# A two-layer hybrid decoder on one core: the first half of a down projection moved into column block 2, with one quad more as seven products

## The chip, the core and the metric

The kernel runs on one core of a Trainium2 chip (trn2). The metric is device time in microseconds of one launch, the median of several runs; lower is better. In the text TensorE is PE, VectorE is DVE, ScalarE is ACT, GpSimd is POOL, and SyncE is SP. Weights reach the core through two DMA queues, one fed by SP and one fed by POOL.

## What is computed

Two layers, each with a token mixer (sparse attention and latent attention side by side, one output projection) and a SwiGLU feed-forward part, each followed by a layer norm. 256 tokens, model width 2048, feed-forward width 5632, all in float32. The change lies in the feed-forward part, which is

```python
def _swiglu(x, w_gate, w_up, w_down):
    h = jax.nn.silu(jnp.einsum('bsd,df->bsf', x, w_gate)) * jnp.einsum('bsd,df->bsf', x, w_up)
    return jnp.einsum('bsf,fd->bsd', h, w_down)

def reference(...):
    for i in range(DEPTH):
        mix = _hybrid_mixer(x, positions, ...)
        x = _layer_norm(ALPHA * x + mix, ln1_g[i], ln1_b[i])
        ffn = _swiglu(x, w_gate[i], w_up[i], w_down[i])
        x = _layer_norm(ALPHA * x + ffn, ln2_g[i], ln2_b[i])
    return x
```

## The kernel before

**Three products for one.** Every float32 operand is split into a high and a low part. A weight unit is a tile of 128 partitions by 1024 (two 128-row steps of K, 512 columns; 512 KB). `load_raw` (L317) brings it in on SP's queue, `parts` makes `wh` from it on ACT (L344) and the remainder `wl` on DVE (L345), and PE takes three products for each pair of token tile and K step: high by high, high by low, low by high. So one unit with one token tile is 2 x 3 = 6 matmuls of 512 columns. There are seven buffers for a pair of `wh` and `wl` in the feed-forward part (`UNITS` 5 and `MORE` 2): unit number n+7 waits until PE has finished with unit n.

**Column blocks.** The feed-forward width is cut into 11 column blocks of 512. Block 0 is computed plainly (`gu`), blocks 1 to 10 by `gate_up`. Gate and up together form a 2 x 2 problem (two token tiles, two column sets), and K is cut into four pairs of units, called quads. A quad is computed in one of three ways, named by a letter in `ORDER`:

- N, `plain_quad`: eight products of 6 matmuls, four units.
- S, `wino_quad`: seven products of 6 matmuls (a Strassen-Winograd scheme). Seven `wh`/`wl` pairs are made; four of them are of sums of weights. One sum is formed by the DMA (`load_sum`: a load and an accumulating load on POOL's queue, L323 and L324), three by DVE (L1049, L1056, L1061). The sums of the activations (tiles `few` and `many`) are made once for a layer.
- Q: seven products with sums that an earlier stage left in HBM.

In the last quad of a block, DVE also joins the products into gate and up (tiles `e` and `g`, L1031). Then `hidden` takes the silu on ACT and the product on DVE (L963), and some units later PE transposes the result (L386); ACT and DVE split it into `hT` (L389, L390).

**Down halves.** The down projection takes column blocks in pairs. `down` computes two of the four output column groups for one pair: 8 units, 96 matmuls. Each finished bank is copied by ACT (tile `d`, L1104) and added to the residual `xt` by an accumulating DMA from POOL's queue (L1105). Before the change, a half stands ahead of each of blocks 3 to 10, the first at block 3 (`FIRSTD`), and two halves stand behind block 10.

**The residual's scaling.** `affine` multiplies and adds the first layer norm's gain and bias to `xt`, one column group at a time: two loads on POOL's queue (L442, L443), two scalings on ACT (L451), four operations of 512 columns on DVE (L453, L454). Group 0 follows the gate of block 0, group 1 the up of block 0, groups 2 and 3 blocks 1 and 2 in the program.

**Who sets the order.** The program's text gives the order of matmuls and of tasks that are stepped as units go by (`spawn`, `tick`, `finish`); the tile framework then schedules each engine's instructions ahead of time, within what the data allow. On the chip every engine works through its list in order.

Of the kernel before, what the change touches and what calls it, by code (L numbers as in the profile page):

```python
# [59 lines left out]
HALF = NKT // KU // 2  # L60
SOONER = 60
SOON = 200
FIRSTD = 3
T2, T2MORE = 4, 6
ALLFROM, EARLY = 4, 0

# [16 lines left out]
def hybrid_trunk(ctx: ExitStack, tc: tile.TileContext, x, xt_in, pos, w_in, g_cq, g_ckv, w_uq,  # L83
# [19 lines left out]
    def turn(name):  # L103
        if phase["cm"] is not None:
            phase["cm"].__exit__(None, None, None)
        phase["cm"] = None
        if name is not None:
            phase["cm"] = tc.tile_pool(name=nm(name), bufs=1)
            phase["pool"] = phase["cm"].__enter__()
        phase["name"] = name  # L110
# [8 lines left out]
    def t2(shape, s, dt=F32):  # L119
        if phase["name"] == "att":  # L120
            phase["t2"] = phase.get("t2", 0) + 1
            if phase["t2"] * T2MORE % (T2 + T2MORE) < T2MORE:
                return pt(shape, dt, s, "t2", T2MORE)
        return sb.tile(shape, dt, name=nm(s), tag="t2", bufs=T2)
# [7 lines left out]
    def bank(i, s):  # L132
        return ps.tile([P, C], F32, name=nm(s), tag=f"b{i}", bufs=1)
# [47 lines left out]
    mhalf = const.tile([P, 1], F32, name="mhalf")  # L181

    make_identity(nc, ident)

    def make_masks():
        cmask, selmask = (pt([P, S], F32, s) for s in ("cmask", "selmask"))
# [102 lines left out]
    def spawn(gen):  # L289
        task = [0, gen]  # L290
        tasks.append(task)
        step(task)
        return task
# [5 lines left out]
    def finish(*ends):  # L299
        while any(e in tasks for e in ends):  # L300
            for task in list(tasks):
                if any(e in tasks for e in ends):
                    step(task)
# [48 lines left out]
    def proj(units, lhs, n, before=None, split_t=None, banks=None):  # L352

        o = [bank(i, "acc") for i in banks] if banks else [acc() for _ in range(NT)]
        loaded = []
        last = len(units) - 1

        def go(t, u):  # L360
            (wh, wl), ks = loaded[u], units[u][1]
            for j, k in enumerate(ks):
                h, l = lhs(t, k)
                a, b = wh[:, j, :n], wl[:, j, :n]
                first, final = u == 0 and j == 0, u == last and j == len(ks) - 1
                mm(o[t][:, :n], h, a, start=first, stop=False)  # L366
                mm(o[t][:, :n], h, b, start=False, stop=False)  # L367
                mm(o[t][:, :n], l, a, start=False, stop=final)  # L368

        for u, (src, ks) in enumerate(units):  # L370
            if before is not None:
                before(u)
            loaded.append(load_unit(src, src.shape[-1]))
            for t in range(1 if split_t else NT):
                go(t, u)
            tick()
        if split_t:
            split_t()
            for u in range(len(units)):
                go(1, u)  # L380
                tick()
        return o
# [156 lines left out]
    def layer(l, xT, norms, last):  # L539
        xk = xlhs(xT)  # L540

        def in_chunk(b, before=None, split_t=None):
            n = IN_BLOCKS[b][1]
            return proj([(w_in[b][l, u], range(u * KU, (u + 1) * KU)) for u in range(NKT // KU)], xk, n,
                        before, split_t)
# [263 lines left out]
        qiT = [qi_whole[:, 0:4, :], qi_whole[:, 4:8, :]]  # L809
        if l == 0:  # L810
            turn("att")
            o = in_chunk(QI0, load_xT)
            nc.gpsimd.memset(mhalf, -0.5)
            make_masks()
            rope_tables()
        else:
            o = in_chunk(QI0, None, lambda: finish(*norms))
            turn("att")
            make_masks()
# [58 lines left out]
        def last_pass(unit, ks, lhs, then):  # L878

            us = []  # L880
            two = many([P, 2, 2, KU * C])
            for c in range(D // C):
                own = two[:, c] if c < 2 else t8([P, 2, KU * C], F32R, "own")
                us.append([load_unit(unit(c, ks[0]), KU * C), parts(load_raw(unit(c, ks[1]), KU * C), KU * C, own)])
            for t in range(NT):
                for c in range(D // C):
                    o = acc()
                    for i, k0 in enumerate(ks):
                        wh, wl = us[c][i]
                        for j in range(KU):  # L890
                            h, lo = lhs(t, k0 + j)
                            mm(o, h, wh[:, j, :], start=i == 0 and j == 0, stop=False)
                            mm(o, h, wl[:, j, :], start=False, stop=False)
                            mm(o, lo, wh[:, j, :], start=False, stop=i == len(ks) - 1 and j == KU - 1)
                        tick()
                    sl = xt[t][:, c * C:(c + 1) * C]
                    with tc.high_priority(offset=SOON):
                        nc.vector.tensor_tensor(sl, sl, o, op=ALU.add)
                then(t)
# [51 lines left out]
        def slhs(name):  # L951
            return lambda k: sums[name, k]

        def hidden(gs, us, hT, wait):

            s = phase["pool"].tile([P, NT, C], F32, name=nm("silu"), tag="silu", bufs=1) if isinstance(gs, list) else gs
            for t in range(NT):
                nc.scalar.activation(s[:, t, :], gs[t] if isinstance(gs, list) else gs[:, t, :], AF.Silu)
            if isinstance(us, list):
                for t in range(NT):  # L960
                    nc.vector.tensor_tensor(s[:, t, :], s[:, t, :], us[t], op=ALU.mult)
            else:
                nc.vector.tensor_tensor(s, s, us, op=ALU.mult)  # L963
            yield wait
            for t in range(NT):
                tp = bank(2 + t, "tr")
                transpose4([s[:, t, j * P:(j + 1) * P] for j in range(4)], tp)
                tv = tp.rearrange("p (k t) -> p k t", k=4)
                split(hT[:, 0, :, t * P:(t + 1) * P], hT[:, 1, :, t * P:(t + 1) * P], tv)
# [6 lines left out]
        def gate_up(fc, order, between):  # L976
# [107 lines left out]
                    between()  # L1084
            return r

        def down_lhs(hTs):
            def lhs(t, k):
                h, j = hTs[k // 4], k % 4
                return h[:, 0, j, t * P:(t + 1) * P], h[:, 1, j, t * P:(t + 1) * P]  # L1090
            return lhs

        def down(pair, cols, between=None):


            fcs, hTs = [h[0] for h in pair], [h[1] for h in pair]
            finish(*[h[2] for h in pair])
            per = C // P // KU
            for i, c in enumerate(cols):
                o = proj([(w_down[l, c, per * fcs[0] + u], range(u * KU, (u + 1) * KU))  # L1100
                          for u in range(per * len(fcs))], down_lhs(hTs), C, None, None, (0, 1) if i % 2 else (2, 3))
                for t in range(NT):
                    d = t2([P, C], "d")
                    nc.scalar.activation(d, o[t], AF.Copy)  # L1104
                    nc.gpsimd.dma_start(xt[t][:, c * C:(c + 1) * C], d, accum_op=ALU.add)  # L1105
                if i == 0 and between:
                    between()

        def behind_ffn(t):
            if last:  # L1110
# [6 lines left out]

        def spawn_hidden(fc, g, u):
            hT = t8([P, 2, 4, S], F32R, "hT")
            wait = 3 if fc + 1 < FIRSTD else 8 if fc + 1 < NFC else 6  # L1120
            held.append((fc, hT, spawn(hidden(g, u, hT, wait))))

        def first_operands():

# [1 line left out]

        def down_half(fc):

            down(held[:2], (0, 1) if fc % 2 else (2, 3), first_operands if fc == ALLFROM else None)
            if fc % 2 == 0:  # L1130
                del held[:2]

        def finish_hidden():
            finish(*[h[2] for h in held])

        ORDER = {1: "NSNS", 2: "NSNS", 3: "SSNS"}
        UNIT = {"NSNS": (0, 2, 1, 3), "SSNS": (1, 2, 0, 3), "SSQS": (1, 2, EARLY, 3)}

        g = gu(0, 0, lambda: finish(*norms))
        affine(ln1_g[l], ln1_b[l], 0, ALPHA)  # L1140
# [3 lines left out]
        spawn_hidden(0, g, u)  # L1144
        for fc in range(1, NFC):
            order = ORDER.get(fc, "SSQS")
            if fc >= FIRSTD:
                down_half(fc)
                finish_hidden()
            g, u = gate_up(fc, [({"N": "plain", "S": "wino", "Q": "made"}[k], v) for k, v in zip(order, UNIT[order])],  # L1150
                           finish_hidden if fc < FIRSTD else None)
            if fc < FIRSTD:
                affine(ln1_g[l], ln1_b[l], fc + 1, ALPHA)
            spawn_hidden(fc, g, u)
        xT, norms, ms = [], [], []
# [1 line left out]
            gb = gains()  # L1157
        else:
            gbT = load_gbT(ln2_T[l])
        down(held[:2], range(D // C))  # L1160
        finish(held[2][2])
        turns["acc"] = 1
        u0 = C // P // KU * (NFC - 1)
        last_pass(lambda c, k: w_down[l, c, u0 + k // KU], [0, KU], down_lhs([held[2][1]]), behind_ffn)
        if last:
            for t in range(NT):
                norm_out(t, gb, ms[t])
# [56 lines left out]
```

## Time and profile before

| what | value |
|---|---|
| runs | 2148.97, 2148.99, 2147.7 us; median 2148.97 |
| the profiled execution | 2150.53 us, of which the span of instructions is 2148.8 |
| granted clock of TensorE, mean | 0.998 of full speed |
| PE busy | 2128.9 us, 99% of the span |
| DVE busy | 1848.4 us, 86% |
| ACT busy | 1292.8 us, 60% |
| POOL busy | 301.7 us, 14% |

Times in rows are microseconds from the start of the span. A timeline row has the start, the duration, the engine, the line, the operation, the tiles (out<-in) and the shapes; a bracket holds the idle time of the engine just ahead of it and what ended that. Matmuls are pipelined: the time that one costs is the distance from its start to the next start, not its duration. DVE's operations overlap a little too, and are read the same way.

### The profile page before, as it was taken

Reading aid. Unit: us, or ns where it says so; the run is one execution under the profiler, and the core shown is the slowest. Engines: PE = TensorE matmul, PEld = TensorE weight load, DVE = VectorE, ACT = ScalarE, POOL = GpSimd, SP = SyncE. Lnnn points to the kernel's source line nnn. Section 1 sums busy time; section 2 is a strip of 40 time slices with the busy share of each in tenths; the row PEclk is TensorE's granted clock in tenths of the full one; section 3 lists DMA queues with packets and bytes.
Section 4 is the critical chain, followed back from the end, with each engine's and each line's share of the span. In section 5 each row is a group of like instructions: output and inputs, shape, how many; then the busy total and the mean of one; then the engine's idle time right before and its main releaser. Section 6 shows DMA issues by size and latency. Waiting matters only on the chain.

```text
span 2148.8 us, 28406 instructions
## 1 busy us (share of the span) xinstructions
PE 2128.9 (99%) x9948; PEld 1769.0 (82%) x9948; DVE 1848.4 (86%) x2361; ACT 1292.8 (60%) x1675; POOL 301.7 (14%) x494
## 2 busy tenths in 40 slices
PE   8999999999999999999999999999999999999997
PEld 7888887888888888888888888888888888888886
DVE  6697776999999999999677976679989999999995
ACT  5555544656676666667555554446666776666663
POOL 0222220010111111110112222200010111111101
PEclk9999999999999999999999999999999999999999
DMA  8687888567888888987656877875687898988993
GB/s 301 209 293 274 304 283 314 169 214 235 262 243 276 274 270 268 292 283 251 204 178 224 294 281 277 314 272 179 206 256 244 277 278 276 275 263 274 298 314 96
DMA packets 158832, 552.97 MB, mean 257 GB/s; under 512 B 17904, under 2 KB 18208, under 8 KB 158048
## 3 DMA queue, kind: packets, MB, share of 16 engines
q1 hardware_dynamic: 111744, 401.79, 53.0%
q0 software_dynamic: 46800, 149.23, 26.1%
q8 instruction: 78, 1.28, 0.2%
q14 instruction: 66, 0.54, 0.1%
q10 hardware_dynamic: 144, 0.13, 0.0%
HBM read 498.12 MB, written 31.46 MB: 246 GB/s over the span
## 4 chain that ended last, share of the span: by engine, by line
PE 87%; DVE 5%; DMA 3%; issue 3%; ACT 1%; POOL 0%; SPq 0%; POOLq 0%; DVEq 0%; ACTq 0%
PE acc L366 15%; PE acc L367 15%; PE acc L368 15%; PE gu_p L992 6%; PE gu_p L995 6%; PE gu_p L994 6%; PE gu_c L992 3%; PE gu_c L995 3%; PE gu_c L994 3%; DMA raw<-in_w_o_dram 2%; PE tr L386 2%; DVE wl L345 2%; PE att L992 2%; PE att L995 2%; PE att L994 2%
## 5 line engine op out<-in xcount | busy, mean ns | idle before, releaser
L344 ACT ACTIVATE wh<-raw 128x1024 fp32r<-128x1024 f32 (+1 forms) x910 | 937.3, 1054 | 574.0 <-PE acc L368 253.4
L345 DVE TENSOR_TENSOR wl<-raw,wh 128x1024 fp32r<-128x1024 f32 (+1 forms) x910 | 1078.9, 1219 | 190.7 <-ACT wh L344 184.3
L366 PE MATMUL acc<-wh,xhl 128*128 128x512 f32 (+1 forms) x768 | 303.1, 396 | 6.2 <-ACT wh L344 6.2
L368 PE MATMUL acc<-wh,xhl 128*128 128x512 f32 (+1 forms) x768 | 297.6, 388 | 0.0
L367 PE MATMUL acc<-wl,xhl 128*128 128x512 f32 (+1 forms) x768 | 297.4, 387 | 0.0
L366 PE MATMUL acc<-wh,hT 128*128 128x512 f32 x640 | 249.3, 389 | 0.0
L368 PE MATMUL acc<-wh,hT 128*128 128x512 f32 x640 | 249.1, 389 | 0.0
L367 PE MATMUL acc<-wl,hT 128*128 128x512 f32 x640 | 249.0, 389 | 0.0
L366 PEld LDWEIGHTS acc<-wh,xhl 128*128 128x128 f32 x768 | 144.7, 189 | 36.6 <-ACT wh L344 7.3
L368 PEld LDWEIGHTS acc<-wh,xhl 128*128 128x128 f32 x768 | 144.6, 188 | 28.3 <-DVE xhl L432 0.6
L367 PEld LDWEIGHTS acc<-wl,xhl 128*128 128x128 f32 x768 | 144.9, 189 | 27.7 <-DVE wl L345 1.9
L367 PEld LDWEIGHTS acc<-wl,hT 128*128 128x128 f32 x640 | 120.1, 188 | 25.2 <-DVE wl L345 0.3
L366 PEld LDWEIGHTS acc<-wh,hT 128*128 128x128 f32 x640 | 120.1, 188 | 25.0 <-DVE hT L390 0.2
L368 PEld LDWEIGHTS acc<-wh,hT 128*128 128x128 f32 x640 | 120.1, 188 | 24.8
L992 PE MATMUL gu_c<-wh,xhl 128*128 128x512 f32 x360 | 140.1, 389 | 0.0
L995 PE MATMUL gu_c<-wh,xhl 128*128 128x512 f32 x360 | 140.1, 389 | 0.0
L994 PE MATMUL gu_c<-wl,xhl 128*128 128x512 f32 x360 | 140.1, 389 | 0.0
L1105 POOL DMA_DIRECT2D x<-d x80 | 68.4, 863 | 367.4 <-ACT d L1104 365.9
L323 POOL DMA_DIRECT2D sum<-in_w_up_dram x56 | 30.9, 552 | 530.6 <-DVE wl L345 498.6
L992 PE MATMUL gu_p<-wh,many 128*128 128x512 f32 x240 | 93.4, 389 | 0.0
L994 PE MATMUL gu_p<-wl,many 128*128 128x512 f32 x240 | 93.4, 389 | 0.0
L995 PE MATMUL gu_p<-wh,many 128*128 128x512 f32 x240 | 93.4, 389 | 0.0
(297 smaller groups left out, 3779.7 us busy)
## 6 DMA issues: line engine op xcount, KB each, us to landing
raw<-in_w_gate_dram SPq DMA_DIRECT2D x176, 512.0 KB, 5.5
raw<-in_w_down_dram SPq DMA_DIRECT2D x176, 512.0 KB, 8.5
raw<-in_w_in_dram SPq DMA_DIRECT2D x144, 512.0 KB, 5.1
sum<-in_w_up_dram POOLq DMA_DIRECT2D x112, 512.0 KB, 7.7
raw<-in_w_up_dram SPq DMA_DIRECT2D x106, 512.0 KB, 5.7
raw<-in_w_o_dram SPq DMA_DIRECT2D x64, 512.0 KB, 6.6
q<-q POOLq DMA_DIRECT2D x56, 512.0 KB, 3.9
raw<-q SPq DMA_DIRECT2D x56, 512.0 KB, 6.3
```

The source lines that it names most:

```text
L323: nc.gpsimd.dma_start(raw, a)
L344: nc.scalar.activation(wh[:, :n], raw[:, :n], AF.Copy)
L345: nc.vector.tensor_tensor(wl[:, :n], raw[:, :n], f(wh[:, :n]), op=ALU.subtract)
L366: mm(o[t][:, :n], h, a, start=first, stop=False)
L367: mm(o[t][:, :n], h, b, start=False, stop=False)
L368: mm(o[t][:, :n], l, a, start=False, stop=final)
L386: nc.tensor.transpose(psum[:, i * P:(i + 1) * P], s, ident)
L992: mm(o[name], h, a, start=name not in begun, stop=False)
L994: mm(o[name], h, b, start=False, stop=False)
L995: mm(o[name], l, a, start=False, stop=end)
L1105: nc.gpsimd.dma_start(xt[t][:, c * C:(c + 1) * C], d, accum_op=ALU.add)
```

## The change

It does three things. The first half of the first pair (blocks 0 and 1) moves from ahead of block 3 into block 2, behind that block's first quad; each later half moves up by one block, so that one half is left behind block 10. The second quad that was plain in block 2 becomes one of seven products: block 2 goes from N S N S to N, the half, S S S. And 22 transposes of the identity stand at the start of the program. With the moved halves, `down` is written anew: it goes through the pair outside and the two column groups inside, holds four banks, and the transposes of the newest hidden values come three units after their block.

```diff
-FIRSTD = 3
+FIRSTD = 2
...
+    def warm_up(n):
+
+        tps = [acc() for _ in range(4)]
+        for i in range(n):
+            nc.tensor.transpose(tps[i % 4][:, :P], ident, ident)
...
             turn("att")
+            warm_up(22)
             o = in_chunk(QI0, load_xT)
...
-                tp = bank(2 + t, "tr")
+                tp = bank(b0 + t, "tr")
...
+        def down(pair, cols, banks, between=None):
+            per = C // P // KU
+            o = {}
+            for w, (fc, hT, task) in enumerate(pair):
+                finish(task)
+                for i, c in enumerate(cols):
+                    if w == 0:
+                        o[c] = [bank(b, "acc") for b in banks[i]]
+                    for u in range(per):
+                        wh, wl = load_unit(w_down[l, c, per * fc + u], KU * C)
...
+                        tick()
...
+                    for t in range(NT) if w else ():
+                        d = t2([P, C], "d")
+                        nc.scalar.activation(d, o[c][t], AF.Copy)
+                        nc.gpsimd.dma_start(xt[t][:, c * C:(c + 1) * C], d, accum_op=ALU.add)
...
-            wait = 3 if fc + 1 < FIRSTD else 8 if fc + 1 < NFC else 6
-            held.append((fc, hT, spawn(hidden(g, u, hT, wait))))
+            held.append((fc, hT, spawn(hidden(g, u, hT, 3, 2 if fc + 1 <= FIRSTD else 4))))
...
-        ORDER = {1: "NSNS", 2: "NSNS", 3: "SSNS"}
+        ORDER = {1: "NSNS", 2: "NSSS", 3: "SSNS"}
...
-            if fc >= FIRSTD:
+            if fc > FIRSTD:
                 down_half(fc)
                 finish_hidden()
...
-                           finish_hidden if fc < FIRSTD else None)
-            if fc < FIRSTD:
+                           finish_hidden if fc < FIRSTD else behind_first if fc == FIRSTD else None)
+            if fc <= FIRSTD:
                 affine(ln1_g[l], ln1_b[l], fc + 1, ALPHA)
...
-        down(held[:2], range(D // C))
-        finish(held[2][2])
+        down_half(NFC)
+        finish_hidden()
```

Lines behind `warm_up` count 6 higher in the changed kernel (L344 becomes L350, L345 L351), those behind `hidden` 7, and those of `down` 15.

**PE at the start.** The first instructions before:

```order
L366 MATMUL acc9_86<-wh13_96,xhl3_68 128x512
L366 MATMUL acc10_87<-wh13_96,xhl5_70 128x512
L367 MATMUL acc9_86<-wl14_97,xhl3_68 128x512
L368 MATMUL acc9_86<-wh13_96,xhl3_68 128x512
L366 MATMUL acc9_86<-wh13_96,xhl3_68 128x512
```

and in the change:

```order
L189 MATMUL acc9_86<-ident_72 128x128
L189 MATMUL acc10_87<-ident_72 128x128
L372 MATMUL acc13_112<-wh17_122,xhl3_68 128x512
L373 MATMUL acc13_112<-wl18_123,xhl3_68 128x512
L374 MATMUL acc13_112<-wh17_122,xhl3_68 128x512
```

Of the 22 transposes (L189) the last two are shown. Behind them one product with `wh`, and not two, now stands ahead of the first that needs `wl`.

**DVE from the last quad of block 2 to the down half behind it, layer 0.** `wl` are remainders of weights; `g` and `e` joinings of products; `x` the residual's scaling. Before, from the sixth product's remainder to the half's second unit:

```order
L345 TENSOR_TENSOR wl1056_4892<-raw1041_4828,wh1055_4891 128x1024
L345 TENSOR_TENSOR wl1058_4904<-raw1042_4830,wh1057_4903 128x1024
L1031 TENSOR_TENSOR g1044_4833<-e1043_4832,gu_c11994_4588 128x512
L345 TENSOR_TENSOR wl1066_4933<-raw1064_4930,wh1065_4932 128x1024
L345 TENSOR_TENSOR wl1069_4951<-raw1067_4948,wh1068_4950 128x1024
```

and in the change, from the fifth product's remainder to the half's first unit (wl1108; the half is now the second of the pair):

```order
L351 TENSOR_TENSOR wl1096_5076<-sum1081_5019,wh1095_5075 128x1024
L1068 TENSOR_TENSOR raw1084_5026<-raw1082_5022,raw1084_5026 128x1024
L1038 TENSOR_TENSOR e1085_5028<-gu_p61054_4896,e1085_5028 128x512
L351 TENSOR_TENSOR wl1098_5088<-raw1083_5024,wh1097_5087 128x1024
L1038 TENSOR_TENSOR e1085_5028<-e1085_5028,gu_p71057_4908 128x512
L351 TENSOR_TENSOR wl1100_5100<-raw1084_5026,wh1099_5099 128x1024
L1038 TENSOR_TENSOR g1086_5029<-gu_c21999_4627,e1085_5028 128x512
L460 TENSOR_TENSOR x2_67<-x2_67,b1102_5111 128x512
L1038 TENSOR_TENSOR e1085_5028<-e1085_5028,att1006_4652 128x1024
L351 TENSOR_TENSOR wl1108_5129<-raw1106_5126,wh1107_5128 128x1024
```

Four joinings (a fifth stands some rows further up) and the last operation of the residual's scaling are ahead of the half's first unit, where one joining was.

**POOL's queue around block 2, layer 0.** `g`, `b` are the gain and bias of the residual's scaling, `sum` a sum of weights, `x<-d` the residual's accumulations. Before:

```order
L442 DMA g985_4562<-in_ln1_g_dram 128x512
L443 DMA b986_4563<-in_ln1_b_dram 128x512
L442 DMA g1059_4914<-in_ln1_g_dram 128x512
L443 DMA b1060_4915<-in_ln1_b_dram 128x512
L323 DMA sum1005_4665<-in_w_up_dram 128x1024
```

and in the change:

```order
L1120 DMA x2_67<-d1032_4806 128x512
L329 DMA sum1081_5019<-in_w_up_dram 128x1024
L1120 DMA x1_66<-d1039_4845 128x512
L448 DMA g1101_5110<-in_ln1_g_dram 128x512
L1120 DMA x2_67<-d1040_4848 128x512
L330 DMA sum1081_5019<-in_w_up_dram 128x1024
L449 DMA b1102_5111<-in_ln1_b_dram 128x512
```

The loads for column group 3 (g1101, b1102) no longer stand ahead of all sums but behind the accumulations of the moved half, and the second behind both loads of the third quad's sum.

## Rows read from the trace of the kernel before

**Rows 1.** The page, busy time of each engine and share of the span.
```profile
PE 2128.9 (99%) x9948; PEld 1769.0 (82%) x9948; DVE 1848.4 (86%) x2361; ACT 1292.8 (60%) x1675; POOL 301.7 (14%) x494
```

**Rows 2.** Timeline of PE: start, duration (both us), instruction; eight products in a row.
```profile
366.15 0.39 PE L893 MATMUL acc<-wl,oA 128*128 128x512 f32 x1
...
367.74 0.39 PE L894 MATMUL acc<-many,oA 128*128 128x512 f32 x1
```

**Rows 3.** Windows, one seven-product quad of block 3: busy us by engine, clock, DMA.
```profile
549.72:559.24 9.52, 9.52 (x44) 7.88 (x42) 9.44 (x9) 7.17 (x8) 1.40 (x2) 1.00 0.66 218
```

**Rows 4.** Timeline of DVE: column block 4, from the first quad to the down half.
```profile
604.93 3.50 DVE L345 TENSOR_TENSOR wl<-raw,wh 128x1024 fp32r<-128x1024 f32 x3
...
615.15 13.71 DVE L345 TENSOR_TENSOR wl<-raw,wh 128x1024 fp32r<-128x1024 f32 x12
628.78 1.22 DVE L1049 TENSOR_TENSOR raw<-sum,raw 128x1024 f32<-128x1024 f32 x1
...
637.45 0.69 DVE L1031 TENSOR_TENSOR e<-gu_p,e 128x512 f32<-128x512 f32 x1
638.05 1.22 DVE L345 TENSOR_TENSOR wl<-raw,wh 128x1024 fp32r<-128x1024 f32 x1
```

**Rows 5.** Timeline of the first 15 us, all engines; [idle before, releaser].
```profile
1.25 0.29 POOL masks.py:199 TENSOR_SCALAR_AFFINE_SELECT ident<-ident 128x128 f32<-128x128 f32 x1
...
6.17 1.22 PE L366 MATMUL acc<-wh,xhl 128*128 128x512 f32 x2 [6.17 <-ACT wh L344]
...
7.43 0.79 PE L367 MATMUL acc<-wl,xhl 128*128 128x512 f32 x1
...
10.16 0.63 PE L368 MATMUL acc<-wh,xhl 128*128 128x512 f32 x1
...
10.18 1.23 DVE L345 TENSOR_TENSOR wl<-raw,wh 128x1024 fp32r<-128x1024 f32 x1 [1.77 <-ACT wh L344]
10.59 0.51 PE L366 MATMUL acc<-wh,xhl 128*128 128x512 f32 x1
...
11.62 0.40 PE L367 MATMUL acc<-wl,xhl 128*128 128x512 f32 x1
```

**Rows 6.** Chain of waits: start, us; one block's eight transposes.
```profile
539.47 0.87 PE tr L386 x8
```

**Rows 7.** Timeline of PE: transposes of column block 1's hidden values, layer 0.
```profile
483.48 0.39 PE L995 MATMUL att<-wh,xhl 128*128 128x512 f32 x1
483.95 0.44 PE L386 MATMUL tr<-ident,g 128*128 128x128 f32 x2
```

**Rows 8.** The same place in layer 1.
```profile
1549.41 0.39 PE L995 MATMUL att<-wh,xhl 128*128 128x512 f32 x1
1550.05 0.55 PE L386 MATMUL tr<-ident,g 128*128 128x128 f32 x3 [0.25 <-DVE g L963]
```

**Rows 9.** Timeline of PE: first use of a remainder in block 5's down half.
```profile
640.71 0.39 PE L367 MATMUL acc<-wl,hT 128*128 128x512 f32 x1
```

**Rows 10.** Timeline, end of the first down half: a product frees a buffer.
```profile
533.64 0.39 PE L368 MATMUL acc<-wh,hT 128*128 128x512 f32 x1
...
534.11 1.06 ACT L344 ACTIVATE wh<-sum 128x1024 fp32r<-128x1024 f32 x1 [1.66 <-PE acc L368]
...
539.51 0.60 ACT L1104 ACTIVATE d<-acc 128x512 f32<-128x512 f32 x1 [0.77 <-PE acc L368]
```

**Rows 11.** Timeline of POOL: a gain's load (layer 0); a sum's second load (block 3).
```profile
439.85 0.54 POOL L442 DMA_DIRECT2D g<-in_ln_g_dram  x1 [2.07 <-DVE x L453]
...
577.30 0.83 POOL L324 DMA_DIRECT2D sum<-in_w_up_dram  x1 [7.55 <-DMA sum<-in_w_up_dram]
```

**Rows 12.** Timeline of ACT: the scaling of that gain.
```profile
443.42 0.63 ACT L451 ACTIVATE g<-g 128x512 f32<-128x512 f32 x1 [0.56 <-DMA g<-in_ln_g_dram]
```

**Rows 13.** Timeline of PE: the longest hole in the layers.
```profile
369.67 0.47 PE L892 MATMUL acc<-wh,oA 128*128 128x512 f32 x1 [1.54 <-DVE x L871]
```

**Rows 14.** Windows, the 2 us in which PE starts again.
```profile
370.00:372.00 2.00, 2.00 (x10) 1.67 (x9) 1.97 (x4) 0.00 (x0) 0.00 (x0) 1.00 0.99 375
```

More of the change, by code (lines that the diff above doesn't have):

```diff
@@ L952, in slhs, with hidden @@
             return lambda k: sums[name, k]
-        def hidden(gs, us, hT, wait):
+        def hidden(gs, us, hT, wait, b0):
             s = phase["pool"].tile([P, NT, C], F32, name=nm("silu"), tag="silu", bufs=1) if isinstance(gs, list) else gs
@@ L1085, in gate_up @@
             return r
+        def down(pair, cols, banks, between=None):
[8 more added lines that the diff above has]
+                        wh, wl = load_unit(w_down[l, c, per * fc + u], KU * C)
+                        for t in range(NT):
+                            for j in range(KU):
+                                h, lo = (hT[:, i, u * KU + j, t * P:(t + 1) * P] for i in range(2))
+                                begin, end = (w, u, j) == (0, 0, 0), (w, u, j) == (1, per - 1, KU - 1)
+                                mm(o[c][t], h, wh[:, j, :], start=begin, stop=False)
+                                mm(o[c][t], h, wl[:, j, :], start=False, stop=False)
+                                mm(o[c][t], lo, wh[:, j, :], start=False, stop=end)
+                        tick()
+                    if w == 0 and i == 0 and between:
+                        between()
+                    for t in range(NT) if w else ():
+                        d = t2([P, C], "d")
+                        nc.scalar.activation(d, o[c][t], AF.Copy)
+                        nc.gpsimd.dma_start(xt[t][:, c * C:(c + 1) * C], d, accum_op=ALU.add)
         def down_lhs(hTs):
@@ L1091, in down_lhs @@
             return lhs
[L1093 to L1107, printed above, removed]
         def behind_ffn(t):
@@ L1127, in down_half, with behind_first @@
         def down_half(fc):
-            down(held[:2], (0, 1) if fc % 2 else (2, 3), first_operands if fc == ALLFROM else None)
-            if fc % 2 == 0:
+            down(held[:2], (2, 3) if fc % 2 else (0, 1), ((0, 1), (2, 3)) if fc == FIRSTD else ((2, 3), (0, 1)),
+                 first_operands if fc == ALLFROM else None)
+            if fc % 2:
                 del held[:2]
+        def behind_first():
+            finish_hidden()
+            down_half(FIRSTD)
         def finish_hidden():
             finish(*[h[2] for h in held])
-        ORDER = {1: "NSNS", 2: "NSNS", 3: "SSNS"}
-        UNIT = {"NSNS": (0, 2, 1, 3), "SSNS": (1, 2, 0, 3), "SSQS": (1, 2, EARLY, 3)}
+        ORDER = {1: "NSNS", 2: "NSSS", 3: "SSNS"}
+        UNIT = {"NSNS": (0, 2, 1, 3), "NSSS": (0, 1, 2, 3), "SSNS": (1, 2, 0, 3), "SSQS": (1, 2, EARLY, 3)}
         g = gu(0, 0, lambda: finish(*norms))
@@ L1159, in layer @@
             gbT = load_gbT(ln2_T[l])
-        down(held[:2], range(D // C))
-        finish(held[2][2])
+        down_half(NFC)
+        finish_hidden()
         turns["acc"] = 1
         u0 = C // P // KU * (NFC - 1)
-        last_pass(lambda c, k: w_down[l, c, u0 + k // KU], [0, KU], down_lhs([held[2][1]]), behind_ffn)
+        last_pass(lambda c, k: w_down[l, c, u0 + k // KU], [0, KU], down_lhs([held[0][1]]), behind_ffn)
         if last:
```

## The prediction

> **What bounds the kernel now.** I read the page first: PE is busy for 99% of the span, DVE for 86% [rows 1]. Then PE's timeline, for the price of a product: seven starts lie between 366.15 and 367.74 us, so a matmul of 512 columns costs 0.227 us, however long its record is [rows 2]. With PE this full, only fewer matmuls, or a new hole, change the time. So the question is who can make PE wait. The window of one seven-product quad answers it: in 9.52 us PE is full and DVE works 9.44 us [rows 3]. DVE is as full as PE where such quads stand; its spare time lies in plain quads and down halves, where a weight unit serves 24 or 12 matmuls instead of 6. DVE's timeline in block 4 shows how close this is: from the first quad to the down half behind it, it works without a hole [rows 4].
>
> **Fewer matmuls.** A plain quad is 8 x 6 = 48 matmuls, one of seven products 42. One quad changes in each of two layers: 12 x 0.227 = **-2.7 us**. The extra unit that its sum loads (512 KB a layer) is hidden: the DMA engines are at 0.66 in the quad's window [rows 3]. Without that cover it would cost the wait for a load.
>
> **The transposes at the start.** Before, the first product starts at 6.17 us at the lower clock: from 10.16 to 10.59, 512 columns take 0.43 us, which is 1.2 GHz; from 10.59 on it rises, with PE at work since 6.17 [rows 5]. The identity is ready at 1.25 + 0.29 = 1.54 us [rows 5], and the transposes run from there. Eight take 0.87 us at the upper clock [rows 6]; 22 take 2.4 us, or 4.8 at half the clock, and end between 4.0 and 6.4 us. Even the later end is hidden, because the first product with `wl` can't start before 7.43 us [rows 5]. What the upper clock gives is small, since the second unit is late: its remainder is done at 10.18 + 1.23 = 11.41 us, and the matmul that needs it started at 11.62 [rows 5]. It can start at 11.43 at best, and from there PE is the slower again: **-0.2 us**.
>
> The rule that speaks against this is in the Trainium skill, TensorE: Matmul & The Clock Gate, "Part 4: PE-mode transpose": transposes don't count as the activity that lifts the clock. No row here has transposes alone, so the trace can't say. By that rule the first unit stays slow. As one product fewer stands ahead of the first `wl`, the unit would end one slow matmul later: +0.4 us in place of -0.2.
>
> **The transposes of block 1.** PE waits ahead of them for DVE's product: 483.48 to 483.95 and 1549.41 to 1550.05 are 0.47 and 0.64 us where 0.23 would do [rows 7, 8]. In the change four small DVE operations (2.4 us, column group 3's scaling) leave block 1, so DVE comes sooner. At most -0.65 us; I take **-0.5**.
>
> **Three quads of seven in a row: a new wait.** I count DVE's list in the changed order, from the first such quad's last remainder (wl1061) to the first remainder of the half behind the third (wl1108). It has 31 operations. Wide ones (1024 columns): that last remainder, ten each for the second and third quad (seven remainders, three sums), the half's first, and one joining: 23. Small ones (512 columns): four joinings and four of the scaling: 8. A wide one costs 13.63 / 12 = 1.136 us (615.15 to 628.78), a small one 0.60 (637.45 to 638.05) [rows 4]. Together 26.1 + 4.8 = 30.9 us.
>
> The same count tested on block 4 of before: 28 wide and 2 small from 604.93 on put the half's first remainder at 637.9; it started at 638.05 and was done at 639.27 [rows 4]. PE used it at 640.71 [rows 9]. So there 1.4 us were left, over four quads of which one has its sums ready.
>
> When does the list start in the change? Let T be the start of the first of the three quads. The operation wl1061 needs the buffer that the down half's last unit frees. In the trace the freeing product starts at 533.64 and ACT follows at 534.11, 0.47 later, for 1.06 us [rows 10]. The product ahead of T starts at T - 0.23, so ACT could begin at T + 0.24, but the copy of the last down bank (0.60 [rows 10]) stands before it in ACT's list. DVE starts at about T + 0.24 + 0.60 + 1.06 = T + 1.9 and is through at T + 32.8. PE needs wl1108 after 3 x 42 products and three pulled ahead, 129 x 0.227 = T + 29.2. PE waits 3.6 us, in two parts, the larger just ahead of the half.
>
> To that come the late loads of column group 3's scaling. ACT scales gain and bias between two units of the second quad, and the units behind them wait. A gain issued at 439.85 is scaled at 443.42, 3.6 us later [rows 11, 12]. In the change POOL issues it behind an accumulation of the half, at about T, so ACT stands until T + 4, a little longer than the buffers would hold it; the bias also stands behind the landing of the third quad's sum. I take 0.5 us for both, so 4.1 a layer. Layer 1 has the same operations: **+8.2 us**. Ends: 3.0 a layer, if the bank's copy costs nothing and the loads are in time; 6.0, if the sum lands as late as in one row, where POOL is idle 7.55 us for it [rows 11]. The value is nearer the lower end because DVE's list alone gives 3.6.
>
> Such holes don't lower the clock: behind a hole of 1.54 us the granted clock is 1.00, the upper level [rows 13, 14].
>
> **Moved work.** The other halves keep their 96 matmuls, 8 loads, 4 copies and 4 accumulations each; POOL, which issues the last, is busy for 14% [rows 1]. A block's transposes, with DVE's part of the split, now stand inside the half that follows, where a unit gives DVE 2.7 us for its 1.14. I cost this at nothing; without that cover a block would lose part of the 1.4 us above. So does the shorter way from block 10 to the final pass, one half in place of two: DVE rests in each unit of it.
>
> **Sum.** -2.7 - 0.2 - 0.5 + 8.2 = +4.8 us. The profiled execution took 2150.53 us (span 2148.8): 2155.3 in its terms. It lies 1.56 above the runs' median of 2148.97, from which I forecast **2153.8 us**. A measurement of this kernel tells about 0.2%, 4.3 us, from no change.
>
> **Rivals.**
> - *DVE keeps up* (not slower). If DVE is 3.6 us further ahead at T than I have it, PE never waits: 2148.97 - 3.4 = 2145.6. For it: DVE has time to spare in the moved half. Against it: seven buffers end its lead, whatever the time. Chance 0.13.
> - *A short wait*, 1 to 3 us a layer, if the copy, the scalings and the joinings fall partly where DVE would stand still anyway: 2147.6 to 2151.6. Chance 0.22.
> - *ACT held by the bias*, 6 to 8 us a layer: 2157.6 to 2161.6. For it: a sum that landed 8 us after its issue; against it: it takes that delay in both layers. Chance 0.11.
> - *The clock stays low at the start*, since the transposes don't lift it: 0.6 us more on any of the others, too little to be a case of its own; an even chance. (This is the skill's rule above.)
>
> **The numbers.** My forecast, 3 to 6 us a layer (2151.6 to 2157.6), has 0.54. The range, 2149.5 to 2158.0, leaves out the case without a wait, part of the short one and most of the longest. Slower by over 0.2% needs more than 3.9 us a layer: rather more than half of my forecast's share, and the longest case, 0.48. Within 0.2% lie the rest of it, the short wait and the case without one, 0.47. Faster by over 0.2% has no case of mine, as all gains come to 3.4 us: 0.05 for what I don't see.
>
> **What would show it.** PE's starts in the changed profile would be whole up to the fifth product of block 2's third quad, then have a wait of 1 to 2 us, and one of 2 to 3 at the next half's first `wl`, both ended by DVE (L351), in both layers, with DVE full since the first of the three quads. Behind 7.43 us matmuls would be 0.227 apart. No hole at the end of block 2 would prove the count wrong; one ended by ACT or a load, with DVE idle, would make the scaling the larger cost; holes in blocks 4 to 10 or the final pass would show that the moved halves aren't free.

## The result: 20 us slower, the loss in one stretch of each layer

| | before | change |
|---|---|---|
| median of 5 runs, us | 2148.99 (2147.7 to 2149.6) | 2169.14 (2168.18 to 2169.86) |
| the profiled execution, us | 2150.53 | 2168.18 |
| its span, us | 2148.8 | 2166.4 |
| PE, DVE busy in the span | [rows 1] | 2138.2 (99%), 1862.6 (86%) |

The ratio is 1.0094, 95% interval 1.0079 to 1.0108: slower. The forecast was 2153.8, its range 2149.5 to 2158.0. The sign was right, and so was the place, block 2 of both layers; the forecast loss of 4.8 us was a quarter of the 20.2 between the medians. The two profiled executions, from which all rows come, lie 17.65 us apart.

Lines of the change to know below: the residual's scaling is L457 on ACT and L459, L460 on DVE, its loads L448 and L449; PE's products of a quad are L999, L1001 and L1002, those of a down half L1111 to L1113.

To see where the time went I add up, for every matmul of 512 columns, how far its successor's start lies beyond 0.227 us, if it does [rows 2]. Call this the excess. In 500 to 555 us (block 2 of layer 0) it rose from 0.1 to 10.4 us, in 1570 to 1645 us (block 2 of layer 1) from 0.1 to 12.9. Nowhere else did it rise by more than 0.2 us; blocks 3 to 10 and the final passes have 2.3 and 0.9 us, as before (2.4 and 1.0). Between 340 and 375 us it fell, from 1.8 to 0.3: the hole of before at 367.74 [rows 13] is not there.

PE's timeline of the change, at the start of block 2's three quads (line L999, called T) and at the holes, in both layers:

```profile
506.98 0.39 PE L999 MATMUL gu_p<-wh,xhl 128*128 128x512 f32 x1
...
520.53 0.39 PE L1002 MATMUL att<-wh,many 128*128 128x512 f32 x1
522.56 0.50 PE L999 MATMUL gu_p<-wh,many 128*128 128x512 f32 x1 [1.64 <-ACT wh L350]
524.61 0.79 PE L1001 MATMUL gu_p<-wl,many 128*128 128x512 f32 x1 [1.55 <-DVE wl L351]
...
544.05 0.40 PE L1002 MATMUL gu_p<-wh,many 128*128 128x512 f32 x1
546.37 0.50 PE L1112 MATMUL acc<-wl,hT 128*128 128x512 f32 x1 [1.92 <-DVE wl L351]
...
1581.76 0.39 PE L999 MATMUL gu_p<-wh,xhl 128*128 128x512 f32 x1
...
1617.54 0.39 PE L1111 MATMUL acc<-wh,hT 128*128 128x512 f32 x1
1620.89 0.80 PE L1112 MATMUL acc<-wl,hT 128*128 128x512 f32 x1 [2.97 <-DVE wl L351]
1621.49 0.63 PE L1113 MATMUL acc<-wh,hT 128*128 128x512 f32 x1
```

The first L1112 of the next half needs the half's first remainder, as the prediction put it. From T to it PE has 129 products, 29.3 us. It took 546.37 - 506.98 = 39.4 us, and 39.1 in layer 1. The forecast had a hole of 2 to 3 us ahead of the half, and one of 1 to 2 us at the fifth product of the second of the three quads, both ended by DVE. The one ahead of the half is there. In the second quad the holes begin a product earlier, at 520.53, they are longer, and the first of them is ended by ACT. So ACT is the next engine to read, in the same stretch:

```profile
515.22 0.63 ACT L457 ACTIVATE g<-g 128x512 f32<-128x512 f32 x1 [5.55 <-issue]
...
520.93 0.63 ACT L457 ACTIVATE b<-b 128x512 f32<-128x512 f32 x1 [3.18 <-issue]
...
1590.21 0.63 ACT L457 ACTIVATE g<-g 128x512 f32<-128x512 f32 x1 [5.76 <-DMA g<-in_ln_g_dram]
```

ACT stands twice ahead of the scaling, 5.55 and 3.18 us. In layer 0 the profile names no releaser ("issue"), in layer 1 it does: the gain's load. On POOL, which issues the loads:

```profile
507.56 0.57 POOL L448 DMA_DIRECT2D g<-in_ln_g_dram  x1
508.28 0.84 POOL L1120 DMA_DIRECT2D x<-d  x1 [0.16 <-issue]
510.57 0.85 POOL L330 DMA_DIRECT2D sum<-in_w_up_dram  x1 [1.45 <-DMA sum<-in_w_up_dram]
511.11 0.88 POOL L449 DMA_DIRECT2D b<-in_ln_b_dram  x1
```

The gain goes out at 507.56 and is scaled at 515.22, 7.7 us later; the bias needs 9.8 us. Before, it was 3.6 [rows 11, 12]. DVE hands the wait on, since the units behind the scaling wait for ACT:

```profile
508.75 2.36 DVE L351 TENSOR_TENSOR wl<-raw,wh 128x1024 fp32r<-128x1024 f32 x2 [1.93 <-ACT wh L350]
515.88 0.69 DVE L459 TENSOR_TENSOR x<-x,g 128x512 f32<-128x512 f32 x1 [4.77 <-ACT g L457]
...
521.60 0.69 DVE L460 TENSOR_TENSOR x<-x,b 128x512 f32<-128x512 f32 x1 [1.26 <-ACT b L457]
...
545.09 1.23 DVE L351 TENSOR_TENSOR wl<-raw,wh 128x1024 fp32r<-128x1024 f32 x1
...
1590.88 0.69 DVE L459 TENSOR_TENSOR x<-x,g 128x512 f32<-128x512 f32 x1 [4.98 <-ACT g L457]
1591.83 2.36 DVE L351 TENSOR_TENSOR wl<-raw,wh 128x1024 fp32r<-128x1024 f32 x2 [0.26 <-ACT wh L350]
...
1595.93 0.69 DVE L460 TENSOR_TENSOR x<-x,b 128x512 f32<-128x512 f32 x1 [0.60 <-ACT b L457]
```

The list starts at 508.75 = T + 1.8, and its last operation, the half's first remainder, is done at 546.3. The windows of the change (the stretch, its length, the busy times of PE, PE's weight loads, DVE, ACT and POOL, the granted clock, the DMA engines' busy share, GB/s) give the sum, and how full the DMA engines are while the gain is under way:

```profile
508.75:546.30 37.55, 31.21 (x122) 23.11 (x121) 31.26 (x32) 22.66 (x26) 4.60 (x7) 0.95 0.70 193
507.00:516.00 9.00, 9.00 (x41) 7.48 (x40) 2.48 (x3) 3.27 (x5) 3.38 (x5) 1.00 1.00 266
```

DVE worked 31.26 us, where 30.9 were forecast, and stood for 37.55 - 31.26 = 6.3 us, in layer 1 for 4.98 + 0.26 + 0.60 = 5.8. The DMA engines' share was 1.00.

### The profile page after: what moved, and what is told of

The parts are those of the page before. It is cut to its first block, busy times and chain, and to the rows that moved or that the text cites. A ratio compares the mean times of both kernels' runs of the same rounds, so it can differ in the third digit from the quotient of the medians.

```text
span 2166.4 us, 28467 instructions
## 1 busy us (share of the span) xinstructions
PE 2138.2 (99%) x9958; PEld 1773.4 (82%) x9958; DVE 1862.6 (86%) x2373; ACT 1295.5 (60%) x1681; POOL 303.4 (14%) x498
## 4 chain that ended last, share of the span: by engine, by line
PE 89%; DVE 6%; issue 3%; DMA 1%; ACT 1%; POOL 1%; SPq 0%; POOLq 0%; DVEq 0%; ACTq 0%
PE acc L372 9%; PE acc L373 9%; PE acc L374 9%; PE acc L1112 7%; PE acc L1113 7%; PE acc L1111 7%; PE gu_p L999 6%; PE gu_p L1002 6%; PE gu_p L1001 6%; PE gu_c L999 3%; PE gu_c L1002 3%; PE gu_c L1001 3%; PE att L1002 2%; PE att L999 2%; PE att L1001 2%
## 5 line engine op out<-in xcount | busy, mean ns | idle before, releaser
L350 ACT ACTIVATE wh<-raw 128x1024 fp32r<-128x1024 f32 (+1 forms) x914 | 941.9, 1053 | 593.4 <-PE acc L374 137.2
L351 DVE TENSOR_TENSOR wl<-raw,wh 128x1024 fp32r<-128x1024 f32 (+1 forms) x914 | 1083.3, 1218 | 214.9 <-ACT wh L350 209.9
L1112 PE MATMUL acc<-wl,hT 128*128 128x512 f32 x640 | 250.5, 391 | 4.9 <-DVE wl L351 4.9
L1111 PE MATMUL acc<-wh,hT 128*128 128x512 f32 x640 | 251.0, 393 | 0.0
L1113 PE MATMUL acc<-wh,hT 128*128 128x512 f32 x640 | 250.5, 391 | 0.0
L1112 PEld LDWEIGHTS acc<-wl,hT 128*128 128x128 f32 x640 | 121.0, 189 | 30.4 <-DVE wl L351 5.7
L1113 PEld LDWEIGHTS acc<-wh,hT 128*128 128x128 f32 x640 | 120.9, 189 | 25.3
L1111 PEld LDWEIGHTS acc<-wh,hT 128*128 128x128 f32 x640 | 120.7, 189 | 24.5
L1001 PE MATMUL gu_c<-wl,xhl 128*128 128x512 f32 x352 | 137.4, 390 | 0.3
L999 PE MATMUL gu_c<-wh,xhl 128*128 128x512 f32 x352 | 137.0, 389 | 0.0
L1002 PE MATMUL gu_c<-wh,xhl 128*128 128x512 f32 x352 | 137.0, 389 | 0.0
L999 PE MATMUL gu_p<-wh,many 128*128 128x512 f32 x240 | 94.8, 396 | 4.2 <-ACT wh L350 4.2
L1001 PE MATMUL gu_p<-wl,many 128*128 128x512 f32 x240 | 95.4, 397 | 3.6 <-DVE wl L351 3.6
L1002 PE MATMUL gu_p<-wh,many 128*128 128x512 f32 x240 | 94.6, 394 | 0.0
L1119 ACT ACTIVATE d<-acc 128x512 f32<-128x512 f32 x80 | 47.7, 596 | 69.1 <-PE acc L1113 68.3
```

The costliest lines, as they stand in the source:

```text
L350: nc.scalar.activation(wh[:, :n], raw[:, :n], AF.Copy)
L351: nc.vector.tensor_tensor(wl[:, :n], raw[:, :n], f(wh[:, :n]), op=ALU.subtract)
L999: mm(o[name], h, a, start=name not in begun, stop=False)
L1001: mm(o[name], h, b, start=False, stop=False)
L1002: mm(o[name], l, a, start=False, stop=end)
L1111: mm(o[c][t], h, wh[:, j, :], start=begin, stop=False)
```

## Theories

- **A.** The late loads hold ACT, ACT holds DVE, and three quads in a row leave no time to make that up.
- **B.** Three quads in a row are too much for DVE anyway; the late loads fill time in which it would stand.

Besides: is it POOL's queue that makes the loads late, what does the moved half cost by itself, and what do the transposes do?

## The experiments

**Scaling early.** Group 3's scaling is called together with group 2's.

```diff
-            if fc <= FIRSTD:
-                affine(ln1_g[l], ln1_b[l], fc + 1, ALPHA)
+            if fc == 1:
+                affine(ln1_g[l], ln1_b[l], 2, ALPHA)
+                affine(ln1_g[l], ln1_b[l], 3, ALPHA)
```

> Column group 3's scaling (two loads, two ACT scalings, four small DVE operations) stands with group 2's, ahead of block 2's three quads; all else as in the change. Theory A (the scaling's late loads hold ACT, ACT holds DVE, 6.3 us of DVE's time a layer): no hole of ACT for g or b in block 2, DVE's list there 30.9 - 2.4 = 28.5 us from T+1.9, so PE waits 30.4 - 29.2 = 1.2 us a layer instead of 10 to 13; time 2149 - 3.2 + 2.4 = about 2148 us, between 2145 and 2151. Theory B (three quads in a row are too much for DVE, late loads only fill time in which it would stand anyway): only the 2.4 us of the small operations go, and with them some slow matmuls: about 2161 to 2165 us.

Measured: 2146.04 us, 0.9985 of before [0.9977, 0.9994]. All of the loss is gone, and the kernel is 0.15% faster than before. The excess in block 2 is 0.3 and 0.2 us. The kernel's timelines of POOL, ACT, DVE and PE:

```profile
437.08 0.54 POOL L448 DMA_DIRECT2D g<-in_ln_g_dram  x1 [2.05 <-DVE x L459]
...
440.76 0.63 ACT L457 ACTIVATE g<-g 128x512 f32<-128x512 f32 x1 [0.58 <-DMA g<-in_ln_g_dram]
...
508.45 3.52 DVE L351 TENSOR_TENSOR wl<-raw,wh 128x1024 fp32r<-128x1024 f32 x3 [1.93 <-ACT wh L350]
...
534.44 1.22 DVE L351 TENSOR_TENSOR wl<-raw,wh 128x1024 fp32r<-128x1024 f32 x1
...
506.67 0.39 PE L999 MATMUL gu_p<-wh,xhl 128*128 128x512 f32 x1
...
535.72 0.50 PE L1112 MATMUL acc<-wl,hT 128*128 128x512 f32 x1
```

The gain is scaled 3.7 us after its issue. DVE starts at T + 1.8 again; the half's first remainder runs at 534.44, is done at 535.66, and PE uses it at 535.72, 29.05 us behind T. Not only the scaling's four operations are gone from the list: with them out, two of the joinings stand behind that remainder instead of ahead of it, so it has 22 wide and 3 small operations, 22 x 1.136 + 3 x 0.60 = 26.8 us. It is just in time; the wait of 1.2 us a layer that I had expected to be left is not there.

**Only the loads early.** Both are loaded ahead of block 2, but scaled and applied inside it. `by` becomes a column that depends on a unit of the second quad.

```diff
+            nc.gpsimd.tensor_scalar(alpha, f(latest["mark"][:, 0:1]), 0.0, by, ALU.mult, ALU.add)
...
+            if fc == 1:
+                early = load_gb(ln1_g[l], ln1_b[l], slice(3 * C, 4 * C))
```

> The change, with column group 3's gain and bias loaded ahead of block 2, but scaled by ACT and applied by DVE inside block 2's second and third quads as in the change (the factor is a number of one column that POOL makes behind the second quad's first unit, so that the scaling can't move up). It takes away the late landing alone and leaves DVE's list. Its list from the first of the three quads' last remainder through the half's first remainder is 24 wide and 8 small operations, 24 x 1.136 + 8 x 0.60 = 32.1 us, from T+1.8, against T+29.2: PE should wait 4.7 us a layer. Theory A (late landing is the larger part of the loss): 2146.0 (scaling early, no wait) + 9.4 = about 2155 us, 2153 to 2158. Theory B (three quads with the scaling among them cost what they cost, and the late loads fill time in which DVE would stand anyway): 2164 to 2169 us, as the change.

Measured: 2160.71 us, 1.0051 [1.0039, 1.0064], between the theories. The timelines of ACT, DVE and PE (lines count 4 or 6 higher in this run):

```profile
507.51 0.60 ACT L1125 ACTIVATE d<-acc 128x512 f32<-128x512 f32 x1 [1.53 <-DMA x<-d]
508.82 0.60 ACT L1125 ACTIVATE d<-acc 128x512 f32<-128x512 f32 x1 [0.72 <-DMA x<-d]
...
510.40 3.50 DVE L351 TENSOR_TENSOR wl<-raw,wh 128x1024 fp32r<-128x1024 f32 x3 [3.17 <-ACT wh L350]
...
541.31 1.22 DVE L351 TENSOR_TENSOR wl<-raw,wh 128x1024 fp32r<-128x1024 f32 x1
...
507.39 0.39 PE L1003 MATMUL gu_p<-wh,xhl 128*128 128x512 f32 x1
...
542.58 0.50 PE L1118 MATMUL acc<-wl,hT 128*128 128x512 f32 x1 [0.64 <-DVE wl L351]
```

DVE now works without a hole from 510.40 to 542.5: 32.1 us, as counted. But it starts at T + 3.0, because two copies of down banks ahead of it on ACT wait for accumulations to land. So the price in layer 0 is 3.0 + 32.1 - 29.3 = 5.8 us, and PE needed 35.2 us from T on, 5.9 too many. In layer 1 it is 37.4 us: there the remainder stands behind all joinings. The early landing alone gave back 2169.1 - 2160.7 = 8.4 us; the other 14.7 lie between this run and the first. They are the list's length and DVE's later start, with slow matmuls behind the holes (starts 0.30 to 0.43 us apart there add 2.1 and 1.3 us of excess). But this run isn't the change less the late landing. Its DVE starts at T + 3.0 in place of T + 1.8, and its list has one wide operation more than the change's 31, together 2.3 us a layer in layer 0. So 8.4 us understates the late landing; with 2 x 2.3 us counted back, an estimate from these rows, it is 13.

**Another queue for the loads.**

```diff
-        nc.gpsimd.dma_start(gc, g[sl].partition_broadcast(P))
+        queue.dma_start(gc, g[sl].partition_broadcast(P))
...
+        gc, bc = load_gb(g, b, sl, nc.scalar if by and c == 3 else nc.gpsimd)
```

> The change, with only column group 3's gain and bias loads issued from ACT's DMA queue in place of POOL's; scaling in the same stretch. Theory A with its cause in POOL's queue (loads stand behind the sums' 512 KB and the accumulations): they land 2 to 4 us after their issue instead of 8, ACT's two stands of 5.6 and 3.2 us go, DVE's list is 30.9 us, PE waits about 3.6 us a layer: 2149 - 3.7 + 7.2 = about 2152.5, up to 2156 if the clock still falls behind the holes. Rival (the DMA engines as a whole are too busy there, or DVE's list alone is too long): loads as late as before or holes as long, 2165 to 2170 us.

Measured: 2165.04 us, 1.0072 [1.0059, 1.0084]. The rival's number. ACT's timeline and that of its queue (ACTq):

```profile
511.27 0.39 ACTq L448 DMA_DIRECT2D g<-in_ln_g_dram  x1
...
513.92 0.34 ACTq L449 DMA_DIRECT2D b<-in_ln_b_dram  x1
...
519.73 0.64 ACT L457 ACTIVATE g<-g 128x512 f32<-128x512 f32 x1 [2.06 <-DMA g<-in_ln_g_dram]
522.91 0.63 ACT L457 ACTIVATE b<-b 128x512 f32<-128x512 f32 x1 [2.54 <-DMA b<-in_ln_b_dram]
```

On a queue of their own they still take 8.5 and 9.0 us. So it isn't what stands ahead of them on POOL's queue. The windows of this run, and of the first experiment where the load took 3.7 us, show the DMA share, 0.94 against 0.53:

```profile
511.00:523.00 12.00, 12.00 (x55) 9.94 (x54) 10.40 (x9) 6.23 (x8) 1.90 (x3) 1.00 0.94 245
...
437.00:441.00 4.00, 4.00 (x23) 3.43 (x22) 3.72 (x5) 3.42 (x6) 1.08 (x2) 1.00 0.53 132
```

The twelve traces hold 288 loads of a gain or a bias, 256 KB each. The 190 with a DMA share below 0.75 between issue and landing took 3.3 to 4.9 us, the 61 with 0.90 or more 5.0 to 10.2; 46 of these stand near 1100 us, far from block 2. So these loads are late wherever the engines are full. That the other transfers are the cause is still argued: no run thins them out. The Trainium skill, DMA: Bandwidth & Descriptors, "Issuing engines are not separate DMA queues", says that all issuers share the same 16 engines. This run agrees: 8.5 us for the gain on ACT's queue, 7.7 on POOL's.

**Third quad plain, scaling late and early.**

```diff
-        ORDER = {1: "NSNS", 2: "NSSS", 3: "SSNS"}
+        ORDER = {1: "NSNS", 2: "NSNS", 3: "SSNS"}
```

> The change, with block 2's third quad plain again (the order of before, 12 matmuls more in all), the half still inside block 2. Theory A: the loads are still late, but behind them stand plain products, 12 matmuls a unit, in which DVE catches up: PE waits at most 2 to 4 us a layer in the second quad, nothing ahead of the next half: 2150 to 2156 us. Theory B (three in a row): no hole at all in block 2: about 2148 us. If moving the half alone did it: holes as in the change, 2165 us or more.

> Scaling behind block 1 as in the first experiment, and block 2's third quad plain again: half moved, transposes added, no further seven-product quad. If moving the half is free by itself and useless without the three quads: the time of before, 2148.7 us (2147.5 to 2149.7), no hole in block 2. If the move gives something by itself, 2146 to 2147.5. If the late scaling was not all that the plain variant with late scaling lost (2156.5 us), 2151 us or more.

Measured: 2156.46 us (1.0033 [1.002, 1.0045]) with the scaling late, 2148.99 (1.0 [0.9991, 1.0009]) with it early, by the first experiment's edit on top of this one. So with a plain quad behind it the late scaling costs 7.5 us, just above the top of what theory A was given, and the moved half with the transposes costs nothing. The four runs make a table:

| us | scaling in block 2 | scaling ahead of it |
|---|---|---|
| third quad plain | 2156.46 | 2148.99 |
| third quad of seven | 2169.14 | 2146.04 |

With the scaling early the further quad gives 3.0 us, about the 2.7 of its matmuls. With the scaling late it costs 12.7. So B falls as I had put it: without the scaling, and with the half ahead of them, DVE keeps up with three quads. A names the right mechanism, but not all of the loss: of the 23.1 us between late and early scaling, the late landing has 8.4 by the run with early loads and about 13 by the estimate from its rows. The rest goes with the scaling's place in DVE's list, where there is no time for four more operations. No run parts the two cleanly.

**Three quads alone.** The kernel before with block 2 as "NSSS".

> The kernel before, with block 2 as one plain quad and three of seven products and nothing else changed: the half stays behind block 2. Theory A (the half's accumulations and sums on POOL's queue delay the loads): without the half the loads land in 3 to 5 us, DVE's list of 30.9 us alone costs 3 to 5 us a layer: 2149 - 2.7 + 8 = about 2154 us, between 2151 and 2157. Theory B (three in a row cost 10 to 13 us a layer wherever the half stands): 2165 to 2170 us. If DVE gets ahead in the plain quad for lack of the half's eight units: 2147 us.

Measured: 2151.69 us, 1.0012 [1.0002, 1.0021]. The number lies in A's interval, but its reason was wrong: without the half the scaling isn't in block 2 at all. It is loaded at 439.71, as before. PE waits all the same (excess 3.1 and 2.1 us), with DVE busy without a hole from 489 to 541 us; its spare time is short of three quads even without the scaling, when no half stands ahead. So the moved half, worth nothing beside a plain quad, is worth 2151.69 - 2146.04 = 5.6 us ahead of three quads of seven (the two runs also differ by the transposes). Its eight units give DVE its lead: in the first experiment DVE stands for 1.93 us just ahead of the quads' list, in the rows there, and here it has no such stand.

**Scaling one block higher.** Group 2 behind block 0, group 3 behind block 1.

> Column group 2's scaling called behind block 0, group 3's behind block 1, all else as in the change. If it is only DVE's list in block 2 that counts, the same time as with both behind block 1: 2146 us (2144.5 to 2147.5). If the scaling's place in block 1 still costs (the wait ahead of block 1's transposes, 0.24 us a layer), up to 0.5 us less. If four more small operations and two loads come in the way of block 1's first units, 2147 to 2149 us.

Measured: 2146.17 us, 0.9988 [0.9979, 0.9997], the same as the first experiment.

**Three quads in block 1 too,** on top of the first experiment.

> As the first experiment (scaling early, 2146.0 us), with block 1 also one plain and three seven-product quads: 12 matmuls fewer, -2.7 us. No half stands ahead of block 1's three quads, as none stood ahead of block 2's in the run that changed only the quads, where PE waited 3.1 and 2.1 us. If a half ahead is what gives DVE its lead, the wait is as long or longer, since block 1 also holds the scaling's small operations (2.4 to 4.8 us): 2.5 to 6 us a layer, 2148 to 2156 us. If any block can take three quads once the scaling is out of block 2: 2143.5 us.

Measured: 2160.97 us, 1.0059 [1.0046, 1.0071]. Worse than expected: the excess in block 1 is 7.9 and 7.7 us. No half stands ahead there, and the scaling is in it; which of the two costs how much, no run shows.

**The transposes.** The change without them, and the kernel before with them.

> The change without the 22 transposes at the start. If they lift the clock (the change's trace has the first unit's products 0.227 us apart from 7.15 us on), the first products should be 0.43 us apart until about 10.6 us, as in the kernel before, and the first stretch ends 0.5 us later: 2169.6 us. If the clock rises without them as soon as products run, no matmul of the first unit is slower: 2169.1 us. If they delayed PE, 2168.5 us.

> The kernel before with the 22 transposes ahead and nothing else. If they lift the clock: products 0.227 us apart from about 7.2 us on, third unit reached 0.2 to 0.5 us sooner, 2148.5 us. If they don't (they aren't the activity that lifts it): 0.43 us apart until about 10.6 us, and 2149 to 2149.4 us.

One run each: 2170.35 and 2148.59 us. Runs of the change alone lie up to 1.7 us apart, so these two times can't tell half a microsecond; PE's rows can. Its first rows without them, in the change:

```profile
9.96 0.63 PE L374 MATMUL acc<-wh,xhl 128*128 128x512 f32 x1
10.39 0.63 PE L372 MATMUL acc<-wh,xhl 128*128 128x512 f32 x1
```

and with them, in the kernel before:

```profile
1.60 4.95 PE L189 MATMUL acc<-ident 128*128 128x128 f32 x22 [1.60 <-POOL ident masks.py:199]
...
7.62 0.40 PE L374 MATMUL acc<-wh,xhl 128*128 128x512 f32 x1
7.86 0.39 PE L372 MATMUL acc<-wh,xhl 128*128 128x512 f32 x1
...
11.72 0.51 PE L373 MATMUL acc<-wl,xhl 128*128 128x512 f32 x1 [0.76 <-DVE wl L351]
```

With them the products are 0.23 us apart from 7.62 us on (2.4 GHz), without them 0.43 (1.2 GHz) until past 10.39. But the first unit is then done early, and PE waits for the second: the excess of the first 50 us falls only from 2.6 to 2.5 in the kernel before, from 2.9 to 2.2 in the change. It isn't safe either. In the run with the other queue the second unit came later, and the clock fell again:

```profile
10.96 0.50 PE L372 MATMUL acc<-wh,xhl 128*128 128x512 f32 x1 [0.98 <-ACT wh L350]
12.22 0.79 PE L373 MATMUL acc<-wl,xhl 128*128 128x512 f32 x1 [0.76 <-DVE wl L351]
12.82 0.63 PE L374 MATMUL acc<-wh,xhl 128*128 128x512 f32 x1
13.24 0.63 PE L372 MATMUL acc<-wh,xhl 128*128 128x512 f32 x1
```

The excess there is 5.0 us; in the other eight traces with transposes it is 1.5 to 3.1, in the three without 2.6 to 3.4.

## Why the prediction was right in direction and too small

- *Fewer matmuls, -2.7.* Holds: 3.0 us between the two early-scaling runs.
- *The transposes, -0.2.* Holds for the change, with 0.1 to 0.7 us of excess less in the two pairs of runs, but no more than by chance (above). Two readings under it were off: in the change the first product with `wl` starts at 7.15, not at 7.43 at the earliest, and the second unit's at 11.00, not 11.43. That the clock stays low, to which I gave an even chance, fell: behind 22 transposes alone the products are 0.23 us apart from 7.62 us on, without them 0.43 until past 10.39. The rule of the Trainium skill, TensorE: Matmul & The Clock Gate, "Part 4: PE-mode transpose", is not borne out for these float32 transposes, which the trace records as MATMUL.
- *Block 1's transposes, -0.5.* Holds: the excess falls by 0.2 and 0.4 us in the two layers.
- *DVE's list.* Holds: start at T + 1.9 forecast, T + 1.8 measured; 30.9 us forecast, 31.26 measured. By the same count this gives 3.6 us of PE's wait.
- ***To that come the late loads: 0.5 us.* This step failed.** The load was priced from a row of a quiet stretch: 3.6 us from issue to scaling [rows 11, 12]. In the new place it took 7.7 to 9.8 us. I had ACT stand until T + 4, with the buffers covering that but for 0.5 us; it stood until 515.22 = T + 8.2, and 1590.21 = T + 8.5 in layer 1, and DVE stood 6.3 and 5.8 us. With the list already 3.6 us too long, every microsecond of DVE's stand is one of PE's: 3.6 + 6.3 = 9.9, measured 39.4 - 29.3 = 10.1 in layer 0 and 9.8 in layer 1. The rival "ACT held by the bias" had the right engine, with 6 to 8 us a layer, and even that was short. Its reason was not what came: POOL stood for the sum only 1.45 us (2.95 in layer 1), and the gain, not the bias, made most of DVE's stand, 4.77 of 6.3 us and 4.98 of 5.8.
- ***Such holes don't lower the clock.* This failed as well,** for 2.8 us of layer 1. In the windows of the change, the hole ahead of the half and what follows:

```profile
1617.50:1620.90 3.40, 0.43 (x3) 0.01 (x2) 3.40 (x5) 2.67 (x4) 0.00 (x0) 0.86 0.92 190
1620.90:1626.60 5.70, 5.70 (x13) 4.47 (x14) 5.70 (x6) 1.03 (x1) 0.00 (x0) 0.50 0.95 297
```

  Behind the hole the granted clock is 0.50, and 13 products are 0.43 us apart, 0.2 each too long. PE alone sets the pace there, so this is lost. The row that I took for proof had one hole of 1.54 us with full work around it [rows 13, 14]; here PE had stood for 3.0 us, with two shorter holes close ahead (1.14 and 0.53 us between two starts, at 1611.05 and 1613.93).

Put in place of the 8.2 forecast, the measured terms are 10.1 + 9.8 + 2.8 = 22.7: 14.5 more. They come from the profiled execution, for which the forecast was 2155.3: 2155.3 + 14.5 = 2169.8, beside a measured 2168.18. Of the 1.6 too many, 1.5 is the hole at 367.74 that is gone, for which the prediction had no term.

The test in the prediction helped only in part. It looked at the end of block 2, where the hole is ended by DVE; the hole ended by ACT, the sign that "would make the scaling the larger cost", stands in the second of the three quads. Half of the loss was there to see: that the order of DMAs had moved the loads into the stretch where the half's accumulations, the sums and the units' loads meet, and that DVE had no time left in it. A price for a full stretch was there too. In the trace of before, POOL issues two biases near 1097 us, at a DMA share of 1.01, and they land after 5.7 and 6.6 us:

```profile
1096.98 1.08 POOL L443 DMA_DIRECT2D b<-in_ln_b_dram  x2
...
1097.30:1103.10 5.80, 5.80 (x28) 4.79 (x27) 5.29 (x10) 2.87 (x4) 0.76 (x2) 1.00 1.01 348
```

## What to carry to other kernels

Price a moved load at the place where it lands, not where it stood: look at the DMA share there, and at what waits in line behind the engine that waits for it. DVE was already the bound on this stretch, and its stands of 6.3 and 5.8 us came through on PE in full. So on such a stretch look first at what else can be moved out of it; here four small operations, two scalings and two loads a layer were worth 23 us. And a change made of several parts can hold a gain: with its scaling ahead of block 2 this one is 0.15% faster than the kernel before.

## What the runs showed that I had not expected

- The gain's load of 256 KB took 3.7 us at a DMA share of 0.53, 7.7 at 1.00 on POOL's queue, and 8.5 at 0.94 on ACT's.
- The clock falls behind some holes and not behind others: it was 0.50 behind the 3.35 us between two starts at 1617.54 in the change, and starts were 0.43 us apart behind two distances of 2.03 and 2.05 us in a row; but in the run with the other queue none were 0.43 us apart behind 2.91 and 1.13 us in a row in layer 0. No length can be read from these runs.
- Near 344 to 368 us, far from the change, the three traces without transposes have a start that is 0.73 to 1.7 us late (before: 1.93 us between two starts at 367.74), and the nine with them at most 0.25. Why, stays open.
